# Two heads side by side by columns: values stationary, weighed and transposed maps moving, in three of the four attentions of a 256-token model

## The chip, the core and the metric

The kernel runs on one core of a Trainium2 chip, as one launch. The metric is the device time of the launch in microseconds (us). TensorE (PE in the profile; PEld is its loading of weights) multiplies matrices, VectorE (DVE), ScalarE (ACT) and GpSimd (POOL) work on elements, and SyncE (SP) issues the loads of the weights. Matrix products are written to PSUM, which has 8 banks of 128 partitions by 512 fp32 values.

## The reference

256 tokens of width 1024 pass through four attentions with two MLPs between them; what matters here are the attentions. In A (8 heads, a top-64 selection of keys), B (8 heads, a forget bias) and C (16 heads, two attentions per head over selected and over windowed keys, and a third over 15 compressed blocks) each head has values of width 64. D, a differential attention with values of width 128, follows.

```python
# A, and B in the same form with other logits
p = masked_softmax(logits, valid)                       # per head, queries x keys
o = einsum('bqhk,bqkr->bqhr', p, values)
# C: three attentions of one head are weighed by learned gates
out = gb[..., 0:1] * o_c + gb[..., 1:2] * o_s + gb[..., 2:3] * o_w
```

With 256 tokens, sequence block 0 (queries 0 to 127) sees 128 keys and block 1 (queries 128 to 255) sees 256 keys. A "map" is the matrix of softmax numerators of one head and one attention: both blocks stand in one tile E of 128 queries by 128 + 256 = 384 keys. A and B have 8 maps each, C has 32 and D has 32.

## The kernel before

All matrix products of the projections and of the MLPs run as three passes of rounded fp32 (a value is split into a rounded part, wH or uH, and a remainder, wL or uL). ACT or DVE rounds each weight tile, DVE makes the remainder; both engines do it all the time, for the weights of whatever comes next. The products inside the attentions run in fp32.

The kernel is not written in the order in which it runs. Each part of the work is a generator (a "strand") that yields one operation at a time; a planner (`_Weaver`) keeps a clock for each engine, takes the strand whose operation can begin first (ties by priority), and emits its instruction, so that each engine's instructions stand in the order of that plan. Where a strand yields a list, such as `[act.copy(...), dve.tensor_copy(...)]`, the planner takes the engine on which it would be done first, after adding a toll to DVE (`TOLL1` and `TOLL2`, 1.8 us each, while A, B and C are planned). That comparison counts the operation which an engine has in hand, not what else waits for that engine. Pools are counted as tokens: 8 PSUM banks (B), 8 tiles E, 2 tiles PT, 4 score tokens S, 14 slots of 4 KB per partition.

An attention runs in this order. `maps_strand` (A, B) and `two_maps` (C) compute the scores of two maps into two banks. In A and B two heads of depth 64 stand side by side by rows of the array (`scores2`). `softmax_num` adds the mask and takes the row minimum on DVE (E, nb), and takes the exponential on ACT, which also sums each row (two instructions, 128x128 and 128x256, each with a read of its accumulator). `pv_part` transposes the map on PE (three 128x128 pieces into a bank), ACT copies it to the tile PT, and three matmuls with a piece of PT stationary and the 64 value columns moving add the output, queries on partitions, to the group's bank `ob`. When all maps of a group are there, `finish` divides by the row sums (in C it also multiplies by the gates and adds the two attentions and the compressed one, `oc`), and `o_strand` transposes the result on PE, rounds it (`slot<-bank` CAST on ACT) and makes the remainder on DVE. The transposed and rounded outputs are what `out_proj` multiplies by the output weights, which it may do row by row as the heads arrive. In A and B the last four rows, in C the last row (`LASTC = 1`), come at the end, piece of the output by piece. After `out_proj` the new residual h is transposed and rounded for the MLP (`u_strand`, `split_cols`).

The names in the profile: L113 is the helper through which every ACT, DVE and POOL instruction is made, L341 a matmul, L339 a transposition; `const` in a transposition is the identity. E, PT and sums are as above, `n` is a half-slot of 512 values, `slot` a slot: queries, keys, values, transposed outputs. An fp32 matmul has two records in the profile, one of rounded fp32 or a transposition one.

Of the kernel before, what the change touches and what calls it, by code (L numbers as in the profile page):

```python
# [18 lines left out]
P = 128  # L19
# [242 lines left out]
def tile_kernel(ctx: ExitStack, tc: tile.TileContext, I: dict, out: bass.AP):  # L262
# [6 lines left out]
    slots = ctx.enter_context(tc.tile_pool(name="slots", bufs=14))  # L269
# [4 lines left out]
    NE, NPT, NS = 8, 2, 4  # L274
    W = _Weaver(B=8, E=NE, PT=NPT, S=NS, slot=14, n2=6, raw=3, w=8, rope=2, dup=3)
# [430 lines left out]

    def pv_part(grp, E, v, o0, o1, ne=1):
# [28 lines left out]

    def maps_strand(grp, qs, ks, evs, masks_of, vs, i, prio, bias=None):
        for e in evs:
            yield ("ev", e)
        yield ("acq", "E", 2)  # L740
        Es = [e384("E", NE) for _ in range(2)]
        masks = yield from masks_of(Es)
        yield ("acq", "S", 2)
        yield ("acq", "B", 2)
        bs = [bank(), bank()]
        yield scores2(bs, qs, ks, bias is None)
        if bias:
            yield T(bias(bs))
        grp.start()

        def free(te):
            W.give("B", te)
            W.give("S", te)

        def one(n):
            E = Es[n]
            yield from softmax_num(E, bs[n][:, 0:P], bs[n][:, P:3 * P], masks[n], grp.sums, 2 * (i + n), free)
            yield from pv_part(grp, E, vs[n], ((i + n) * P, (i + n) * P + 64), ((i + n) * P + 64, (i + n + 1) * P))

        W.spawn(one(1), prio + 1, W.end + 0.2)  # L760
        yield from one(0)
# [165 lines left out]
    def layer_ab(pl, hin, hout):  # L927
# [212 lines left out]
        def attention(qT, kT, v, evs, masks_of, bias, side, prio):  # L1140
            for g in range(2):
                def finish(grp, g=g):
                    rs = small(8, "rs", 4)
                    yield dve.reciprocal(out=rs, in_=grp.sums)
                    yield ("acq", "n2")
                    on = n2()
                    te = yield dve.tensor_tensor(
                        out=on.rearrange("p (t h d) -> p h t d", t=2, h=4),
                        in0=grp.ob.rearrange("p (h t d) -> p h t d", h=4, t=2),
                        in1=rs.rearrange("p (h t) -> p h t", h=4).unsqueeze(3).to_broadcast([P, 4, 2, 64]),  # L1150
                        op=ALU.mult)
                    W.give("B", te)
                    yield from o_strand(lambda j, t: on[:, t * S + j * P:t * S + (j + 1) * P],
                                        oH[side][:, 2 * g:2 * g + 2, :], oL[side][:, 2 * g:2 * g + 2, :],
                                        oev[4 * side + 2 * g:4 * side + 2 * g + 2])

                grp = Group(4, finish)
# [46 lines left out]
    def layer_c(pl, hin, hout):  # L1204
# [185 lines left out]
        def cmp_att(g, Q, qev, oc, ocev):  # L1390
# [23 lines left out]
            summed = W.end  # L1414
            rc = small(16, "crc", 2)
            rcev = _Event()

            def sums():
                yield dve.tensor_reduce(out=sc, in_=e3, axis=AX.X, op=ALU.add)
                yield dve.tensor_scalar(out=sc, in0=sc, scalar1=1e-30, scalar2=None, op0=ALU.max)  # L1420
                yield dve.reciprocal(out=sc, in_=sc)
                yield ("ev", gev)
                te = yield dve.tensor_tensor(out=rc.rearrange("p (t h) -> p t h", t=2),
                                             in0=sc.rearrange("p (t h) -> p t h", t=2),
                                             in1=gates[:, :, 8 * g:8 * g + 8, 0], op=ALU.mult)
                rcev.set(te)

            W.spawn(sums(), 8 + 20 * g, summed)
            yield ("acq", "B")
            b = bank()  # L1430
            te = yield T([tr(b[:, t * P:(t + 1) * P], ec[:, t * P:(t + 1) * P]) for t in range(2)])
            yield ("acq", "n2")
            pt = n2()[:, :S]
            te = yield [act.copy(pt, b[:, :S]), dve.tensor_copy(pt, b[:, :S])]
            W.give("B", te)
            yield ("ev", rcev)
            W.give("n2", W.now)
            for t in range(2):
                yield ("acq", "B")
                b = bank()  # L1440
                yield T([mm(b, pt[:, t * P:(t + 1) * P], vBD[g].rearrange("p h d -> p (h d)"), True, True)])
                te = yield dve.tensor_tensor(out=heads(oc[:, t, :]), in0=heads(b),
                                             in1=rc[:, 8 * t:8 * t + 8].unsqueeze(2).to_broadcast([P, 8, 64]),
                                             op=ALU.mult)
                W.give("B", te)
            W.give("n2", te)
            ocev.set(te + 0.16)

        def group(g):
            yield ("acq", "slot", 3)  # L1450
            Q, qev = [kslot(slot(F32R)) for _ in range(2)], [_Event(2), _Event(2)]
            oc = slot().rearrange("p (t n) -> p t n", t=2)
# [34 lines left out]
            ocev = _Event()  # L1487
            W.spawn(cmp_att(g, Q, qev, oc, ocev), 8 + 20 * g)

            def two_maps(grp, q_, j):  # L1490
                for e in qev + kev[0] + kev[1] + vev[0] + vev[1]:
                    yield ("ev", e)
                yield ("acq", "E", 2)
                yield ("acq", "S")
                yield ("acq", "B", 2)
                b1, b0 = bank(), bank()
                yield T([mm(b1, q_[:, P:S], k_[:, g], i == 0, i == 1) for i, k_ in enumerate((kH, kL))]
                        + [mm(b0[:, 0:S], q_[:, 0:P], k_[:, g, :, 0:P], i == 0, i == 1)
                           for i, k_ in enumerate((kH, kL))])
                grp.start()  # L1500
                freed = _Event(2)

                def free(te):
                    freed.set(te)
                    if freed.t is not None:
                        W.give("B", freed.t, 2)
                        W.give("S", freed.t)

                def one(y):
                    E = e384("E", NE)  # L1510
                    yield from softmax_num(E, b0[:, y * P:(y + 1) * P], b1[:, y * S:(y + 1) * S], causal, grp.sums,
                                           4 * j + 2 * y, free)
                    i = 2 * j + y
                    yield from pv_part(grp, E, [vsw[:, t, y, 64 * g:64 * g + 64] for t in range(2)],
                                       (i * P, i * P + 64), (i * P + 64, (i + 1) * P))

                W.spawn(one(1), grp.prio + 2 * j + 1, W.end + 0.2)
                yield from one(0)

            def finish_of(hp):  # L1520
                def finish(grp):
                    rs = small(8, "rs", 4)
                    yield dve.reciprocal(out=rs, in_=grp.sums)
                    yield ("ev", gev)
                    hd = 8 * g + 2 * hp
# [23 lines left out]
            for hp in range(4):  # L1549
                grp = Group(4, finish_of(hp))  # L1550
                grp.prio = 10 + 20 * g + 4 * hp
                for j in range(2):
                    W.spawn(two_maps(grp, Q[j][:, hp, :], j), grp.prio + 2 * j)
# [301 lines left out]
```

## Time and profile before

| | |
|---|---|
| time, three runs | 924.33 to 925.85 us, median 925.32 |
| the profiled execution | 921.53 us, its span 919.4 us |
| PE busy | 901.2 us, 98% of the span |
| DVE, ACT, POOL busy | 586.6, 518.2, 106.4 us |
| mean granted clock of TensorE | 0.998 |

The trace belongs to one execution, 3.8 us below the median of the three runs. Times in it count from the span's start. A's and B's maps are made from about 91 to 130 us, C's from 380 to 457 us, D's from 693 us on. A row of the timeline merges like instructions that follow each other: start, length of the whole row, engine, line, operation, tiles and shapes, count. The start of the next row is a better measure of what a row costs than its own length, since the next instruction begins before the last one's result is written.

### The profile page before, as it was taken

What the parts mean: (1) busy time and instruction counts of PE and PEld (TensorE: products, weight loads), DVE (VectorE), ACT (ScalarE), POOL (GpSimd) and SP (SyncE); (2) the same over time, 40 slices, a digit from 0 to 9 for tenths busy, and PEclk for the clock granted to TensorE, in tenths of its full rate; (3) what the DMA queues carried; (4) which work ended last, traced back from release to release, by engine and by line L of the source; (5) the groups of instructions that cost most, each with busy time, mean ns of one, the idle gap of its engine ahead of it and who ended that gap; (6) DMA issues with size and microseconds to landing.
All of it is one profiled execution on the core that took longest, in us unless ns stands there. A gap on an engine that the chain in (4) does not pass through costs nothing.

```text
span 919.4 us, 14126 instructions
## 1 busy us (share of the span) xinstructions
PE 901.2 (98%) x5196; PEld 766.9 (83%) x5196; DVE 586.6 (64%) x1230; ACT 518.2 (56%) x1025; POOL 106.4 (12%) x149
## 2 busy tenths in 40 slices
PE   8999999999999999999999999999999999999998
PEld 6778888999999878888789999998877778777786
DVE  5688646544454457766654445444878878697781
ACT  5666858455544564787575544455637545274450
POOL 3520000000000051120000000000310503204000
PEclk9999999999999999999999999999999999999999
DMA  7756134655555474312236665655674545544431
GB/s 233 207 178 211 55 104 164 203 183 187 189 191 190 133 249 143 110 46 70 74 123 196 208 192 179 198 184 161 161 220 130 159 138 160 165 133 159 140 115 46
DMA packets 65124, 144.55 MB, mean 157 GB/s; under 512 B 7214, under 2 KB 9744, under 8 KB 65056
## 3 DMA queue, kind: packets, MB, share of 16 engines
q1 hardware_dynamic: 63632, 140.68, 48.0%
q0 software_dynamic: 1424, 2.98, 1.6%
q8 instruction: 41, 0.67, 0.3%
q14 instruction: 27, 0.22, 0.1%
HBM read 142.59 MB, written 1.05 MB: 156 GB/s over the span
## 4 chain that ended last, share of the span: by engine, by line
PE 86%; DVE 4%; POOL 4%; DMA 3%; ACT 1%; issue 1%; SPq 0%; POOLq 0%; DVEq 0%; ACTq 0%
PE bank L341 81%; PE bank L339 5%; POOL qrs L113 2%; DVE wL L113 2%; DVE n L113 1%; DMA h<-in_x_dram 1%; ACT wH L113 1%; DMA raw<-in_c_w_in_dram 1%; POOL T L113 1%; POOL drn L113 1%; DMA raw<-in_ab_w_in_dram 1%; DVE qss L113 0%; DMA raw<-in_l_w_in_dram 0%; ACT n L113 0%; DVE dss L113 0%
## 5 line engine op out<-in xcount | busy, mean ns | idle before, releaser
L113 DVE TENSOR_TENSOR wL<-raw,wH 128x1024 fp32r<-128x1024 f32 (+2 forms) x262 | 317.8, 1214 | 187.9 <-ACT wH L113 186.2
L113 ACT CAST wH<-raw 128x1024 fp32r<-128x1024 f32 (+2 forms) x226 | 234.8, 1041 | 225.4 <-PE bank L341 181.4
L341 PE MATMUL bank<-wH,slot 128*128 128x512 f32 (+1 forms) x784 | 258.3, 396 | 1.2 <-ACT slot L113 0.6
L341 PE MATMUL bank<-wH,uH 128*128 128x512 f32 (+2 forms) x448 | 182.8, 408 | 0.5 <-ACT uH L113 0.5
L341 PE MATMUL bank<-wH,uL 128*128 128x512 f32 (+2 forms) x448 | 174.9, 390 | 0.0
L341 PE MATMUL bank<-wL,uH 128*128 128x512 f32 (+2 forms) x448 | 174.6, 390 | 0.0
L341 PEld LDWEIGHTS bank<-wH,slot 128*128 128x128 f32 x784 | 147.2, 188 | 32.1 <-issue 1.7
L341 PE MATMUL bank<-wL,slot 128*128 128x512 f32 (+1 forms) x392 | 152.7, 390 | 0.0
L341 PE MATMUL bank<-uH,wL 128*128 128x256 f32 x448 | 127.4, 284 | 0.0
L341 PE MATMUL bank<-uL,wH 128*128 128x256 f32 x448 | 127.0, 284 | 0.0
L341 PE MATMUL bank<-uH,wH 128*128 128x256 f32 x448 | 126.1, 281 | 0.0
L341 PEld LDWEIGHTS bank<-wH,uH 128*128 128x128 f32 x448 | 85.1, 190 | 20.2 <-issue 2.3
L341 PEld LDWEIGHTS bank<-wH,uL 128*128 128x128 f32 x448 | 84.8, 189 | 18.7 <-DVE uL L113 0.4
L341 PEld LDWEIGHTS bank<-wL,uH 128*128 128x128 f32 x448 | 85.2, 190 | 15.0 <-DVE wL L113 0.2
L341 PEld LDWEIGHTS bank<-uH,wH 128*128 128x128 f32 x448 | 85.0, 190 | 0.6
L341 PEld LDWEIGHTS bank<-uL,wH 128*128 128x128 f32 x448 | 84.3, 188 | 0.6
L341 PEld LDWEIGHTS bank<-wL,slot 128*128 128x128 f32 x392 | 73.8, 188 | 13.0
L341 PEld LDWEIGHTS bank<-uH,wL 128*128 128x128 f32 x448 | 84.6, 189 | 0.0
L113 ACT ACTIVATE E<-E,nb 128x128 f32<-128x128 f32 (+1 forms) x160 | 70.8, 447 | 9.7 <-DVE nb L113 9.6
L113 POOL TENSOR_TENSOR qrs<-qss,neghalf 128x8 f32<-128x8 f32 x16 | 36.3, 2272 | 141.6 <-DVE dss L113 110.0
L341 PEld LDWEIGHTS bank<-slot,PT 128*128 128x128 f32 x384 | 48.7, 191 | 3.9 <-issue 0.7
L113 POOL TENSOR_TENSOR r<-ms,neghalf 128x1 f32<-128x1 f32 x6 | 4.0, 668 | 403.3 <-DVE ms L113 403.3
(206 smaller groups left out, 953.4 us busy)
## 6 DMA issues: line engine op xcount, KB each, us to landing
raw<-in_mlp_w_dram SPq DMA_DIRECT2D x128, 512.0 KB, 3.9
raw<-in_l_w_in_dram SPq DMA_DIRECT2D x64, 512.0 KB, 3.8
raw<-in_ab_w_in_dram SPq DMA_DIRECT2D x16, 512.0 KB, 4.1
raw<-in_l_w_out_dram SPq DMA_DIRECT2D x16, 512.0 KB, 3.4
raw<-in_c_w_in_dram SPq DMA_DIRECT2D x12, 512.0 KB, 4.0
raw<-in_ab_w_out_dram SPq DMA_DIRECT2D x8, 512.0 KB, 3.4
raw<-in_c_w_out_dram SPq DMA_DIRECT2D x8, 512.0 KB, 3.5
slot<-in_ab_w_in_dram SPq DMA_DIRECT2D x8, 256.0 KB, 6.2
```

The source lines that it names most:

```text
L113: return _Op(self.key, self.cost(name, a, kw), lambda: f(*a, **kw), bank[0] if bank else None)
L339: i = pe.transpose(c[0], c[1], ident[:c[2], :c[2]])
L341: i = pe.matmul(c[0], lhsT=c[1], rhs=c[2], start=c[3], stop=c[4], skip_group_check=True)
```

## The change

It concerns A, B and C; D keeps `pv_part`.

- **The product with the values.** `pv_pair` takes the two maps of two heads (in C: of one attention) together. Their transposed maps are the moving operand (256 columns for the first 128 keys, with both blocks' queries, and 128 columns for the last keys), and the 64 value columns are stationary. Head 0 uses columns 0 to 63 of the array and head 1 columns 64 to 127, so that the output has the head's dimensions on partitions and the queries along the free axis. It is thus already transposed.
- **The division.** Rows are queries in E, but columns in the new output, so the map must be divided before it is transposed: `weigh` multiplies each map by the reciprocal of its row sums (in C also by the gate), two instructions per map, on ACT or DVE. In C the compressed attention's map is weighed too, and its product with the values (`vBD`, 8 matmuls of 256 columns for 4 of 512) is added into the same bank.
- **The end of a group.** `o_round` rounds the bank and takes the remainder; the transposition, the multiplication by reciprocals and, in C, the additions are gone. In C a group now has two pairs of heads, and its end releases two rows of `out_proj` at once (for one before).
- **Buffers.** 4 tiles PT for 2, 13 slots for 14, and C uses no slot for the compressed output.

```diff
-    slots = ctx.enter_context(tc.tile_pool(name="slots", bufs=14))
+    slots = ctx.enter_context(tc.tile_pool(name="slots", bufs=13))
-    NE, NPT, NS = 8, 2, 4
+    NE, NPT, NS = 8, 4, 4
+    def weigh(E, w, ready):
+        for j, (a, z) in enumerate(HALVES):
+            yield [act.activation(out=E[:, a:z], in_=E[:, a:z], func=AF.Copy, scale=w[:, j:j + 1]),
+                   dve.tensor_scalar(out=E[:, a:z], in0=E[:, a:z], scalar1=w[:, j:j + 1], scalar2=None, op0=ALU.mult)]
+        ready.set(W.end + 0.13)
+
+    def pv_pair(grp, Es, ready, vs, col, prio, more=None):
...
+        def across(n):
+            yield ("ev", ready[n])
+            yield ("acq", "B")
+            b = bank()
+            te = yield T([tr(b[:, j * P:(j + 1) * P], Es[n][:, j * P:(j + 1) * P]) for j in range(3)])
+            W.give("E", te)
+            te = yield [act.copy(PTs[n], b[:, :384]), dve.tensor_copy(PTs[n], b[:, :384])]
...
+            o = grp.ob[:, col:col + S]
+            hi = [slice(0, 64), slice(64, 128)]
+            return ([mm(o[hi[n], :], vs[n][0], PTs[n][:, 0:S], first, False) for n in range(2)]
+                    + [mm(o[hi[n], P:S], vs[n][1], PTs[n][:, S:S + P], False, last) for n in range(2)])
+        te = yield T(calls, 2)
...
+        if more:
+            te = yield T([mm(grp.ob[:, col:col + S], more[1], more[2](), False, False)])
...
+    def o_round(grp, H, L, evs):
+        bv = grp.ob.rearrange("p (j q) -> p j q", j=2)
+        yield [act.copy(H, bv), dve.tensor_copy(H, bv)]
+        te = yield dve.tensor_tensor(out=L, in0=bv, in1=H.bitcast(F32), op=ALU.subtract)
...
     def maps_strand(...):     # A, B
+            w = small(2, "w2", 8)
+            yield dve.reciprocal(out=w, in_=sums[:, 2 * n:2 * n + 2])
+            yield from weigh(E, w, ready[n])
...
-                grp = Group(4, finish)
+                grp = Group(2, finish)
...
     def maps_of(grp, hp, prio):     # C, in place of two_maps
+                    w = small(4, "w4", 8)
+                    yield dve.reciprocal(out=w, in_=sums)
+                    yield dve.tensor_tensor(out=wv, in0=wv, op=ALU.mult, in1=gates...)
+                    W.spawn(weigh(Es[1][j], w[:, 2:4], ready[1][j]), prio + 2 * j + 1, W.end + 0.13)
+                    yield from weigh(Es[0][j], w[:, 0:2], ready[0][j])
```

Counted over the whole program, PE loses 144 matmuls `slot,PT` of 64 columns, 32 transpositions `const,n` and 4 matmuls `slot,n` of 512 columns; it gains 48 matmuls `PT,slot` of 256 columns and 48 of 128 columns, each on 64 columns of the array, and 8 matmuls `n,slot` of 256. ACT gains 48 instructions `E<-E,w` of 128x128 and 48 of 128x256: every weighing is on ACT, none on DVE. ACT's 8 casts `slot<-bank` of 128x256 become 4 of 128x512. DVE loses 12 multiplications of 128x512 from the ends of the groups, 4 of the compressed output, and most of the additions, and gains small reciprocals.

PE in the first part of C, before (E and PT are maps, plain and transposed; n_4084 is the compressed attention's transposed map, n_4124 a finished output on its way to be transposed):

```order
L339 MATMUL bank<-const,E 128x128 x6
L341 MATMUL bank<-slot 128x512 x2
L341 MATMUL bank<-slot 128x256 x2
L341 MATMUL bank<-slot,n_4084 128x512
L341 MATMUL bank<-slot,PT 128x64 x6
L339 MATMUL bank<-const,E 128x128 x3
L339 MATMUL bank<-const,n_4124 128x128 x2
```

And in the changed kernel, the same engine and place:

```order
L339 MATMUL bank<-const,E 128x128 x6
L341 MATMUL bank<-slot 128x512 x2
L341 MATMUL bank<-slot 128x256 x2
L341 MATMUL bank<-PT,slot 64x256 x2
L341 MATMUL bank<-PT,slot 64x128 x2
L341 MATMUL bank<-n_4125,slot 128x256
L341 MATMUL bank<-PT,slot 64x256 x2
L341 MATMUL bank<-PT,slot 64x128 x2
```

The six matmuls of a pair of maps have become four, the transposition of the finished output is gone, and the compressed product stands between two pairs.

ACT in the first part of C, before:

```order
L113 ACTIVATE E,sums<-E,nb 128x128
L113 ACTIVATE E,sums<-E,nb 128x256
L113 COPY PT<-bank 128x384 x2
L113 COPY n_4084<-bank 128x256
L113 ACTIVATE E,sums<-E,nb 128x128
L113 ACTIVATE E,sums<-E,nb 128x256
```

ACT in the changed kernel there (w_4143 holds a head's reciprocals times its gates):

```order
L113 ACTIVATE E,sums_4007<-E,nb 128x128
L113 ACTIVATE E,sums_4007<-E,nb 128x256
L113 ACTIVATE slot<-bank 64x4x128 x4
L113 COPY PT<-bank 128x384 x2
L113 ACTIVATE E<-E,w_4143 128x128 x2
L113 ACTIVATE E<-E,w_4143 128x256 x2
L113 ACTIVATE E,sums_4027<-E,nb 128x128
L113 ACTIVATE E,sums_4027<-E,nb 128x256
```

Four weighings (two maps) have come in between the copies of one pair and the exponentials of another. In A and B 32 such instructions are added, in C 64.

PE at the end of C, before (wH,slot and wL,slot are `out_proj`):

```order
L341 MATMUL bank<-slot,PT 128x64 x6
L341 MATMUL bank<-wH,slot 128x512
L341 MATMUL bank<-wL,slot 128x512
L341 MATMUL bank<-wH,slot 128x512 x2
L341 MATMUL bank<-wL,slot 128x512
L341 MATMUL bank<-wH,slot 128x512
L339 MATMUL bank<-const,n_4907 128x128 x2
L341 MATMUL bank<-wH,slot 128x512
```

PE at the end of C in the changed kernel:

```order
L339 MATMUL bank<-const,E 128x128 x12
L341 MATMUL bank<-PT,slot 64x256 x2
L341 MATMUL bank<-PT,slot 64x128 x2
L341 MATMUL bank<-n_4471,slot 128x256
L341 MATMUL bank<-PT,slot 64x256 x2
L341 MATMUL bank<-PT,slot 64x128 x2
L341 MATMUL bank<-wH,slot 128x512
L341 MATMUL bank<-wL,slot 128x512
L341 MATMUL bank<-wH,slot 128x512 x2
```

Before, 6 of `out_proj`'s matmuls stand between the last product and the last transposition, and 12 behind it, with the transpositions of h between them. In the changed kernel all that is left, 24 matmuls, stands behind the last product, and then 16 transpositions of h in one piece. At the end of A and B, 57 matmuls of `out_proj` stand behind the last transposition of an output before, and 42 behind the last product in the changed kernel. Of the rounding casts of weights, ACT has 7 between the first exponential of A and the last cast of B for 5 before, and 6 in that stretch of C for 9 before. Between the end of A's selection mask and the first exponential there is one cast of weights on ACT for two before.

## Rows read from the trace of the kernel before

**Rows 1.** The page's part 1: busy us, share of the span, instructions.
```profile
PE 901.2 (98%) x5196; PEld 766.9 (83%) x5196; DVE 586.6 (64%) x1230; ACT 518.2 (56%) x1025; POOL 106.4 (12%) x149
```
**Rows 2.** Busy time by window: stretch, length, PE, PEld, DVE, ACT, POOL, clock, DMA.
```profile
90.70:129.90 39.20, 39.20 (x279) 33.35 (x278) 23.10 (x94) 29.90 (x91) 0.00 (x0) 1.00 0.22 67
380.30:457.30 77.00, 74.96 (x508) 65.47 (x507) 53.82 (x210) 58.82 (x187) 7.81 (x14) 1.00 0.19 62
380.30:394.30 14.00, 13.99 (x98) 12.07 (x98) 12.18 (x62) 13.71 (x56) 0.73 (x1) 1.00 0.12 39
```
**Rows 3.** Timeline of PE in C: start, length, engine, line, operation, count.
```profile
395.59 1.45 PE L341 MATMUL bank<-slot,PT 128*128 128x64 f32 x12
396.88 0.83 PE L339 MATMUL bank<-const,E 128*128 128x128 f32 x6
397.46 0.94 PE L341 MATMUL bank<-slot 128*128 128x512 f32 x4
```
**Rows 4.** Timeline of PE in B, and at the end of `out_proj`.
```profile
106.21 0.93 PE L341 MATMUL bank<-slot 64*128 64x128 f32 x8
107.07 0.62 PE L341 MATMUL bank<-cumk,slot 72*128 72x384 f32 x2
...
143.49 0.39 PE L341 MATMUL bank<-wH,uH 128*128 128x512 f32 x1
143.72 0.39 PE L341 MATMUL bank<-wL,uH 128*128 128x512 f32 x1
```
**Rows 5.** Timeline of ACT in C.
```profile
386.26 0.39 ACT L113 ACTIVATE E<-E,nb 128x128 f32<-128x128 f32 x1
386.56 0.19 ACT L113 ACTIVATION_READ_ACCUMULATOR E<-E,nb 128x1 f32 x1
386.65 0.49 ACT L113 ACTIVATE E<-E,nb 128x256 f32<-128x256 f32 x1
387.05 0.19 ACT L113 ACTIVATION_READ_ACCUMULATOR E<-E,nb 128x1 f32 x1
387.14 0.83 ACT L113 COPY PT<-bank 128x384 f32<-128x384 f32 x2
387.87 0.38 ACT L113 COPY n<-bank 128x256 f32<-128x256 f32 x1
388.13 0.41 ACT L113 ACTIVATE E<-E,nb 128x128 f32<-128x128 f32 x1
```
**Rows 6.** ACT's groups, 380.3 to 457.4 us: busy, mean ns, idle before, releaser.
```profile
L113 ACT CAST wH<-raw 128x1024 fp32r<-128x1024 f32 x9 | 9.4, 1045 | 3.9 <-PE bank L341 3.7
L113 ACT CAST slot<-bank 128x256 fp32r<-128x256 f32 x8 | 2.9, 368 | 1.9 <-PE bank L339 1.8
L113 ACT ACTIVATE slot<-bank 64x512 fp32r<-64x512 f32 x4 | 2.4, 590 | 1.8 <-PE bank L339 1.7
L113 ACT ACTIVATE n<-bank,r 128x512 f32<-128x512 f32 x2 | 1.4, 684 | 0.2 <-PE bank L341 0.2
L113 ACT ACTIVATE n<-n 128x256 f32<-128x256 f32 x2 | 0.8, 414 | 0.2 <-DVE n L113 0.2
L113 ACT COPY n<-bank 128x256 f32<-128x256 f32 x2 | 0.7, 374 | 1.1 <-PE bank L339 1.1
```
**Rows 7.** ACT's groups, 90.7 to 129.95 us.
```profile
L113 ACT CAST slot<-bank 128x512 fp32r<-128x512 f32 x4 | 2.3, 582 | 0.1
```
**Rows 8.** Timeline of ACT at the start of A's exponentials.
```profile
88.05 1.05 ACT L113 CAST wH<-raw 128x1024 fp32r<-128x1024 f32 x1 [1.74 <-DVE slot L113]
90.72 0.40 ACT L113 ACTIVATE E<-E,nb 128x128 f32<-128x128 f32 x1 [1.62 <-DVE nb L113]
```
**Rows 9.** Timeline of all engines behind C: the last cast, and PE.
```profile
456.97 0.36 ACT L113 CAST slot<-bank 128x256 fp32r<-128x256 f32 x1
...
458.71 0.73 PE L341 MATMUL bank<-wH,slot 128*128 128x512 f32 x2 [0.59 <-DVE slot L113]
...
464.43 0.50 PE L341 MATMUL bank<-wH,uH 128*128 128x512 f32 x1 [0.51 <-ACT uH L113]
```

More of the change, by code (lines that the diff above doesn't have):

```diff
@@ L273, in tile_kernel @@
     psum = ctx.enter_context(tc.tile_pool(name="psum", bufs=8, space=PSUM))
[L274 to L275 removed]
+    NE, NPT, NS = 8, 4, 4
+    W = _Weaver(B=8, E=NE, PT=NPT, S=NS, slot=13, n2=6, raw=3, w=8, rope=2, dup=3)
     act, dve, pool = _Engine("A", nc.scalar), _Engine("D", nc.vector), _Engine("P", nc.gpsimd)
@@ L705, in start, with calls @@
                 self.sums = small(8, "sums", 6)
+    def weigh(E, w, ready):
[4 more added lines that the diff above has]
+    def pv_pair(grp, Es, ready, vs, col, prio, more=None):
+        yield ("ev", ready[0])
+        yield ("acq", "PT", 2)
+        PTs = [e384("PT", NPT) for _ in range(2)]
+        there = _Event(2)
+        def across(n):
[5 more added lines that the diff above has]
+            te = yield [act.copy(PTs[n], b[:, :384]), dve.tensor_copy(PTs[n], b[:, :384])]
+            W.give("B", te)
+            there.set(te + 0.2)
+        W.spawn(across(1), prio + 0.1, W.now)
+        yield from across(0)
+        yield ("ev", there)
+        if more:
+            yield ("ev", more[0])
+        if not grp.opening:
+            grp.opening = True
+            yield ("acq", "B")
+            grp.ob = bank()
+            grp.opened.set(W.now)
+        else:
+            yield ("ev", grp.opened)
+        def calls():
+            first, last = grp.done == 0, grp.done == grp.n - 1
+            o = grp.ob[:, col:col + S]
[3 more added lines that the diff above has]
+        te = yield T(calls, 2)
+        W.give("PT", te, 2)
+        if more:
+            te = yield T([mm(grp.ob[:, col:col + S], more[1], more[2](), False, False)])
+            more[3](te)
+        grp.done += 1
+        if grp.done == grp.n:
+            W.spawn(grp.finish(grp), FIN, te + 0.2)
@@ L735, in pv_part @@
             W.spawn(grp.finish(grp), FIN, te + 0.2)
[L737 to L761, printed above, removed]
     def o_strand(nat, H, L, evs, gp=None, width=2):
@@ L1142, in finish @@
                 def finish(grp, g=g):
[L1143 to L1155, printed above, removed]
-                grp = Group(4, finish)
+                    yield from o_round(grp, oH[side][:, 2 * g:2 * g + 2, :], oL[side][:, 2 * g:2 * g + 2, :],
+                                       oev[4 * side + 2 * g:4 * side + 2 * g + 2])
+                grp = Group(2, finish)
                 for j in (0, 2):
@@ L1492, in two_maps @@
                     yield ("ev", e)
[L1493 to L1515, printed above, removed]
@@ new lines, in maps_of @@
+                W.spawn(head(1), prio + 2, W.now)
+                for y in range(2):
+                    vs = [[vsw[:, t, y, 64 * g:64 * g + 64] for t in range(2)]] * 2
+                    more = None
+                    if y == 0:
+                        more = (pcev, vBD[g][:, 2 * hp:2 * hp + 2, :].rearrange("p h d -> p (h d)"), lambda: pc[0], used)
+                    W.spawn(pv_pair(grp, Es[y], ready[y], vs, (hp % 2) * S, prio + y, more), prio + y)
+                yield from head(0)
@@ L1561, in layer_c @@
         yield from out_proj(pl["out"], opnd, lambda k: oev[k], residual(hout), LASTC)
-        W.give("slot", W.end, 14)
+        W.give("slot", W.end, 12)
     def plan_d():
```

141 lines of the change are left out of this document (81 added, 60 removed).

## The prediction

> **What bounds the kernel now.** I read the page's busy shares first, then windows of the two stretches that the change touches, then the timelines of PE and ACT inside them, and last ACT's groups. The shares show PE busy for 98% of the span, DVE for 64%, ACT for 56% [rows 1]. Over the whole program ACT looks like an engine with much room. The windows show something else. While A's and B's maps run (90.7 to 129.9 us) PE is busy all 39.20 us, and ACT 29.90; while C's run, PE is busy 74.96 of 77.00 us and ACT 58.82; in the first 14 us of C, ACT is busy 13.71, as full as PE [rows 2]. The clock is 1.00 in all of them, so it plays no part. PE sets the time in both stretches, but ACT has only 9.3 and 18.2 us left, and the change takes work from PE and hands it to ACT. Two steps follow: what PE saves, and whether ACT can pay.
>
> **PE's step.** A pair of maps now takes twelve records of 64 moving columns, from 395.59 to 396.88, 1.29 us; the six transpositions behind them take 0.58, 0.097 each [rows 3]. There are 24 pairs, so 24 x 1.29 = 31.0 us go, and 32 transpositions of outputs with 32 x 0.097 = 3.1 us. What comes is 24 pairs of two matmuls of 256 columns and two of 128, each on half of the array's columns. The trace has no halves by columns. It has a pair with the same moving shapes in halves by rows: eight records, 0.86 us [rows 4]. Bounds: a pass of 512 columns costs 0.23 us [rows 4]. If the halves overlap wholly, four passes of 128 + 256 = 384 columns cost 4 x 384/512 x 0.23 = 0.69; if they follow each other, and each half has the overhead of the row halves, it is twice 0.86, 1.72. I take 0.86, the row with the same shapes: 24 x 0.86 = 20.6 us. The compressed product, 8 matmuls of 256 columns for 4 of 512, costs the same. The sum is 20.6 - 31.0 - 3.1 = -13.5 us, if PE remains what is waited for.
>
> The halves by rows run beside each other, since 0.86 lies far nearer to 0.69 than to 1.72 [rows 4]. The Trainium skill says so too (TensorEngine Tiling (Array Packing), Key Properties), and adds that changing the tiling mode drains TensorE; by that the excess over 0.69 would be the drain. The same page's section PSUM Bottleneck speaks against the change: tiling speeds TensorE but not the emptying of what it writes, for which both ScalarE and VectorE should be used. Here all 96 weighings go to one of them, and ACT's 13.71 of 14.00 us is what this rule looks like in a row [rows 2].
>
> **ACT's step.** A map costs ACT at present two exponentials with their reads, 386.26 to 387.14, 0.88 us, and one copy to PT, half of 387.14 to 387.87, 0.37 us [rows 5]. New is the weighing: two instructions of 128x128 and 128x256 from tile to tile. The trace has no multiplication of that form. The nearest rows are the exponentials of the same shapes, tile to tile with an operand per partition: 0.30 and 0.40 us to the start of their reads [rows 5], 0.70 together. A lower bound is the copy of 128x256, 387.87 to 388.13, 0.26 us [rows 5], which with a smaller one of about half makes 0.40; an upper one the exponentials with their reads, 0.88. I take 0.70, the shape, route and operand being the same.
>
> By the Trainium skill (ScalarE: Activation LUTs, What ACT_TABLE_LOAD costs) a pass can be built from a fixed part, a part per element and one per pointer operand; my estimate from its figures is 0.29 + 0.40 = 0.69 us per map, so the trace's 0.70 agrees and the sum stays. Its section Rules for kernel authors gives multiplications to VectorE, the opposite of what the order does here; no row of before shows a weighing there.
>
> So a map will cost 0.88 + 0.37 + 0.70 = 1.95 us.
>
> - A and B: 16 maps x 1.95 = 31.2; 7 casts of weights of 1.05 [rows 8] = 7.4; 4 casts of outputs of 0.58 = 2.3 [rows 7]; two banks of 128x512 scaled by an operand per partition, 1.4 as the two of that form in C [rows 6]. Sum 42.3 us, for a stretch of 39.2.
> - C: 32 x 1.95 = 62.4; 6 casts x 1.05 = 6.3; 4 roundings of 128x512 at 0.58 = 2.3 for the eight of 0.37; 2.4 for the four of 64x512; 1.4 + 0.8 + 0.7 = 2.9 for the compressed maps [rows 6]. Sum 76.3 us, for a stretch of 77.0.
>
> ACT becomes the bound in both. It will not be full to the last: where it is full today 0.29 of 14.00 us, 2.1%, stay idle [rows 2], 0.9 and 1.6 us. At the end of a stretch nothing is left to it but to wait for the last pair: six transpositions (0.58) and a product (0.86), 1.4 us. So 2.3 us idle in A and B, 3.0 in C.
>
> **Where the waits go.** ACT works in order. Four weighings now stand before the exponentials of the next maps [the order at the start of C]. Those exponentials empty no bank (E is a tile), but the transpositions of their maps wait for them and then for their own weighing, and the copies to PT, which give banks back, wait behind both. PE has the next scores and `out_proj` to fill in with, until banks or E run out; then it stands, for ACT, about as long as the change saves it. DVE, with 53.82 of 77.00 us [rows 2], loses work and is not waited for more than now.
>
> **Sum by place.**
> - A and B: one cast fewer stands before the first exponential (two from before 88.05 to 90.72 now, 1.05 each [rows 8]), so it starts 1.1 us earlier. The last cast comes at 42.3 + 2.3 - 39.2 - 1.1 = +4.3 us. Behind it 42 matmuls of `out_proj` stand for 57, 15 x 0.23 = 3.5 us less [rows 4]. Net +0.8.
> - C: the last cast comes at 76.3 + 3.0 - 77.0 = +2.3 us. Behind it stand 24 matmuls for 12, as the last group releases two rows: 12 x 0.23 = +2.8. The remainder on DVE is of twice the columns; PE waits 0.59 for it today [rows 9], and I add 0.2, the difference between the two sizes of cast. The way from the last cast to the MLP's first matmul, 456.97 + 0.36 to 464.43, is 7.1 us [rows 9] and becomes 10.1. Net +5.3.
> - D, the MLPs: their instructions stand as before but for small shifts: 0. One slot fewer and two PT more: 0 while PE is not the bound. If slots were short, the weights' loads would be late, which I leave in the range.
>
> That is +6.1 us: 921.5 + 6.1 = 927.6 for the profiled execution. It lies 3.8 us below the median of the runs, so the time is 931.4 us.
>
> **Rivals.**
> 1. *ACT keeps up.* Casts of weights, of which there are 13 in the two stretches, yield to the maps, and ACT's idle 9.3 and 18.2 us [rows 2] take the weighings as they are. Then PE stays the bound and the time is 925.3 - 13.5 = 911.8. For it: the small share of ACT on the page. Against it: 16 and 32 maps x 0.70 = 11.2 and 22.4 us are more than ACT has free. It decides if a map's weighing costs under about 0.3 us, or if ACT's other work moves to DVE. Chance 0.13. This is the one on the other side.
> 2. *The weighing is cheap.* At 0.40 a map ACT needs 37.5 and 66.7 us. The last casts come at 37.5 + 0.8 + 1.4 - 39.2 - 1.1 = -0.6 and 66.7 + 1.4 + 1.4 - 77.0 = -7.5; with -3.5 and +3.0 behind them the sum is -8.6, the time 916.7. For it: the copy of 0.26 us. Against it: the copy has no operand per partition. Chance 0.13.
> 3. *The column halves do not run beside each other.* The change then does not do what it says: a pair costs 1.72, PE 24 x 1.72 - 34.1 = +7.2 us; PE is the bound again, and with the +3.0 behind C the time is 935.5. For it: no row shows halves by columns, and both write the same bank. Against it: the row halves. Chance 0.12.
>
> **How the numbers follow.** The forecast has 0.62. Its own range is 925 to 940: below by the idle ends being filled and 24 matmuls partly hidden (6 us), above by 0.88 us a weighing, 48 x 0.18 = 8.6 us more. What a measurement of this kernel can tell from no change is about 0.2%, 1.85 us, so 923.5 to 927.2 count as the same. Faster: rivals 1 and 2 and a sliver of the forecast, 0.27. Same: 0.11, from the forecast's low end and between the cases. Slower: 0.62. For 8 in 10 I take 915 to 941, which holds rival 2 at its price and rival 3, and leaves out rival 1.
>
> **What will show it.** ACT should be busy for nearly all of both stretches, and PE idle there behind PT's copies and the weighed E, for 10 us or more in all. The weighings should cost 0.30 and 0.40 us from start to start, a pair's product 0.86, the last cast of C should come near 459.3 us and the MLP's first matmul 10 us behind it. I am wrong in PE's step if a product of a pair takes over 1.3 us; in ACT's price if a map's weighing takes under 0.5; in the bound if PE is still busy over 97% of both stretches; and in the ends if the gap behind C's last cast stays near 7 us.

## The result and the profile after

The changed kernel takes 932.07 us (931.45 to 936.38, 5 runs) against 924.55 us of before (922.24 to 925.85, 5 runs). The ratio is 1.009, 95% interval 1.0062 to 1.0118: slower by 6 to 11 us. The forecast was 931.4 us, +6.1 us. The profiled execution of the changed kernel took 936.38 us, 4.3 above its median; a second profile, of 931.79 us, is among the experiments.

The page of the changed kernel, busy us, share of the span and instructions, to be read against [rows 1]:

```profile
PE 903.5 (97%) x5076; PEld 751.8 (80%) x5076; DVE 578.0 (62%) x1223; ACT 547.9 (59%) x1116; POOL 100.5 (11%) x143
```

On the page alone little has happened: ACT has 30 us more, PE is as busy as before in a longer span. The windows of the two stretches tell more (stretch, length, PE, PEld, DVE, ACT, POOL, clock, DMA share and GB/s, as in [rows 2]), from A's first exponential to the end of B's last cast, and the same in C:

```profile
90.19:136.10 45.91, 41.91 (x254) 28.84 (x252) 24.63 (x104) 42.07 (x125) 0.00 (x0) 1.00 0.21 69
389.00:468.85 79.85, 71.47 (x423) 52.71 (x422) 41.44 (x191) 75.93 (x244) 3.25 (x8) 0.96 0.10 31
```

ACT has become the fullest engine in both: 42.07 of 45.91 and 75.93 of 79.85 us. PE, full before, has holes, and DVE is busy for half the time. (PE's 41.91 us in A and B are close to ACT's, but they are not what PE needs there: with the weighing on DVE, below, 248 records take 37.89 us for these 254.) In C the DMA share has fallen from 0.19 to 0.10. That fits ACT's six casts of weights there for nine; with the weighing on DVE the share is 0.19 again. Two groups of ACT in C, the new weighings (busy, mean ns of one, idle before):

```profile
L113 ACT ACTIVATE E<-E,w 128x256 f32<-128x256 f32 x32 | 14.7, 505 | 0.0
L113 ACT ACTIVATE E<-E,w 128x128 f32<-128x128 f32 x32 | 11.3, 403 | 0.3 <-DVE w L113 0.2
```

ACT's timeline late in C (start, length of the row, count), where four weighings, two maps, start at 463.05 and the next instruction at 464.45:

```profile
463.05 1.51 ACT L113 ACTIVATE E<-E,w 128x128 f32<-128x128 f32 x4
464.45 1.05 ACT L113 CAST wH<-raw 128x1024 fp32r<-128x1024 f32 x1
```

That is 1.40 us for two maps, 0.70 a map. On PE a pair's product, the form that no row of before had, stands between 459.35 and 460.15:

```profile
459.35 0.87 PE L341 MATMUL bank<-PT,slot 128*64 128x256 f32 x8
460.15 0.70 PE L341 MATMUL bank<-n,slot 128*128 128x256 f32 x2
```

0.80 us for eight records, where twelve took 1.29 [rows 3] and the halves by rows 0.86 [rows 4]. What PE waited for in A's and B's stretch, and then in C's (us in total, times, longest):

```profile
PE bank L341 <- ACT PT L113: 1.5, 2, 1.0
PE bank L339 <- ACT E L113: 1.3, 2, 0.7
PE bank L341 <- ACT slot L113: 0.3, 1, 0.3
```
```profile
PE bank L339 <- DVE n L113: 2.7, 1, 2.7
PE bank L339 <- ACT E L113: 2.1, 4, 1.1
PE bank L341 <- ACT PT L113: 1.6, 3, 1.0
PE bank L341 <- DVE slot L113: 1.2, 2, 0.8
```

Before, PE was busy all of A's and B's stretch [rows 2], and in C it waited for this:

```profile
PE bank L341 <- ACT PT L113: 0.6, 1, 0.6
PE bank L339 <- DVE slot L113: 0.5, 1, 0.5
PE bank L339 <- DVE n L113: 0.4, 1, 0.4
```

Now five of the seven rows name ACT, with 6.8 of 10.7 us, 6.5 of them for the weighed E and its copy PT. The longest single wait, though, 2.7 us near the start of C, is for DVE and the compressed attention's map n, which the change divides before it is transposed.

Behind A and B, PE meets something that the forecast did not have. Its timeline, in part, from its first wait at the end of B on:

```profile
128.89 0.44 PE L339 MATMUL bank<-const,E 128*128 128x128 f32 x2 [0.68 <-ACT E L113]
...
130.42 0.86 PE L341 MATMUL bank<-PT,slot 128*64 128x256 f32 x6 [0.52 <-ACT PT L113]
...
132.47 0.44 PE L339 MATMUL bank<-const,E 128*128 128x128 f32 x2 [0.60 <-ACT E L113]
133.87 1.25 PE L341 MATMUL bank<-PT,slot 128*64 128x256 f32 x8 [0.96 <-ACT PT L113]
136.15 0.79 PE L341 MATMUL bank<-wH,slot 128*128 128x512 f32 x1 [1.03 <-ACT slot L113]
136.74 0.63 PE L341 MATMUL bank<-wL,slot 128*128 128x512 f32 x1
...
139.82 0.63 PE L341 MATMUL bank<-wL,slot 128*128 128x512 f32 x1
140.25 0.63 PE L341 MATMUL bank<-wH,slot 128*128 128x512 f32 x1
140.68 1.05 PE L339 MATMUL bank<-const,h 128*128 128x128 f32 x4
```

A pass of 512 columns takes 0.43 us (from 139.82 to 140.25, and to 140.68), not the 0.23 of [rows 4]: the granted clock is 0.78 on the mean of 130 to 140 us, so part of it ran at 1.2 GHz instead of 2.4. Ahead of it stand PE's waits of 0.5 to 1.0 us from 128 us on.

Behind C, the timelines of PE, of DVE and of ACT:

```profile
475.13 0.39 PE L341 MATMUL bank<-wH,slot 128*128 128x512 f32 x1
477.60 2.45 PE L339 MATMUL bank<-const,h 128*128 128x128 f32 x16 [2.07 <-DVE h L113]
481.02 0.50 PE L341 MATMUL bank<-wH,uH 128*128 128x512 f32 x1 [0.97 <-ACT uH L113]
```
```profile
474.35 2.59 DVE L113 TENSOR_TENSOR wL<-raw,wH 128x1024 fp32r<-128x1024 f32 x2 [1.64 <-ACT wH L113]
476.86 2.48 DVE L113 TENSOR_TENSOR h<-bank,h 128x512 f32<-128x512 f32 x4
```
```profile
473.27 1.05 ACT L113 CAST wH<-raw 128x1024 fp32r<-128x1024 f32 x1 [1.81 <-DMA raw<-in_mlp_w_dram]
474.63 1.05 ACT L113 CAST wH<-raw 128x1024 fp32r<-128x1024 f32 x1 [0.31 <-DMA raw<-in_mlp_w_dram]
```

PE is done with `out_proj` at 475.5, but DVE has two remainders of weights in front of the residuals h, and those had waited for ACT's casts of weights. Four such casts stand behind C's last cast of an output, where before there was none, and they wait for their weights to arrive, 4.2 us in all. So h begins at 476.86 and PE's 16 transpositions at 477.60.

### The profile page after: what moved, and what is told of

It reads as the page before. It is cut to its first block, busy times and chain, and to the rows that moved or that the text cites. A ratio compares the mean times of both kernels' runs of the same rounds, so it can differ in the third digit from the quotient of the medians.

```text
span 934.3 us, 13917 instructions
## 1 busy us (share of the span) xinstructions
PE 903.5 (97%) x5076; PEld 751.8 (80%) x5076; DVE 578.0 (62%) x1223; ACT 547.9 (59%) x1116; POOL 100.5 (11%) x143
## 3 DMA queue, kind: packets, MB, share of 16 engines
q1 hardware_dynamic: 63632, 140.68, 47.4%
## 4 chain that ended last, share of the span: by engine, by line
PE 84%; ACT 5%; DVE 4%; POOL 3%; DMA 2%; issue 2%; SPq 0%; POOLq 0%; ACTq 0%
PE bank L341 79%; PE bank L339 4%; ACT E L113 2%; ACT wH L113 1%; POOL qrs L113 1%; DMA raw<-in_mlp_w_dram 1%; DVE wL L113 1%; POOL T L113 1%; DVE n L113 1%; DMA h<-in_x_dram 1%; DMA raw<-in_c_w_in_dram 1%; ACT n L113 1%; ACT PT L113 1%; ACT slot L113 0%; DVE E L113 0%
## 5 line engine op out<-in xcount | busy, mean ns | idle before, releaser
L341 PEld LDWEIGHTS bank<-uL,wH 128*128 128x128 f32 x448 | 84.3, 188 | 0.6
L113 POOL TENSOR_TENSOR qrs<-qss,neghalf 128x8 f32<-128x8 f32 x16 | 33.9, 2122 | 142.2 <-DVE dss L113 110.3
L341 PE MATMUL bank<-slot 64*128 64x128 f32 (+3 forms) x288 | 39.8, 348 | 0.3 <-ACT PT L113 0.3
```

The source lines that it names most:

```text
L113: return _Op(self.key, self.cost(name, a, kw), lambda: f(*a, **kw), bank[0] if bank else None)
L341: i = pe.matmul(c[0], lhsT=c[1], rhs=c[2], start=c[3], stop=c[4], skip_group_check=True)
```

## The experiments

The theory going in: ACT's list is what PE waits for (theory 1). Its rivals: the ends of the stretches cost the time wherever the weighing runs (theory 2), or DVE would be the next bound (theory 3). Every ratio is to the kernel before, run on the same chip. The table gives, from the profile of each kernel, the way from the first exponential to the end of the last cast of an output, and from there to the MLP's first matmul, for A with B and for C, in us.

| kernel | median us | ratio (95%) | A, B | behind | C | behind |
|---|---|---|---|---|---|---|
| before | 924.55 | | 39.2 | 13.6 | 77.0 | 7.1 |
| forecast | 931.4 | | 44.6 | 10.1 | 79.3 | 10.1 |
| changed | 932.07 | 1.009 (1.006 to 1.012) | 45.9 | 14.4 | 79.9 | 12.2 |
| changed, again | 931.92 | 1.0103 (1.008 to 1.013) | 45.8 | 14.5 | 79.6 | 12.1 |
| weighing on DVE | 912.27 | 0.9882 (0.986 to 0.990) | 37.9 | 12.4 | 70.1 | 8.7 |
| no weighing | 911.15 | 0.9871 (0.985 to 0.989) | 37.4 | 13.1 | 67.5 | 8.7 |
| weighing halved | 919.12 | 0.9967 (0.994 to 0.9995) | 40.1 | 11.7 | 75.5 | 8.7 |
| C row by row | 931.0 | 1.0082 (1.006 to 1.010) | 46.0 | 13.2 | 79.8 | 9.1 |
| DVE, row by row | 914.05 | 0.9896 (0.986 to 0.993) | 37.9 | 12.4 | 73.2 | 6.2 |
| PE kept busy | 930.54 | 1.0071 (1.005 to 1.009) | 45.9 | 12.0 | 77.6 | 11.8 |
| C only | 936.01 | 1.0143 (1.012 to 1.017) | 46.4 | 12.7 | 77.2 | 11.8 |
| C only, 14 slots, 2 PT | 936.29 | 1.0127 (1.011 to 1.015) | 39.2 | 13.6 | 84.3 | 10.5 |
| changed, 14 slots, 2 PT | 936.13 | 1.0134 (1.011 to 1.016) | 43.4 | 12.1 | 84.5 | 12.1 |
| DVE, 14 slots, 2 PT | 918.37 | 0.9944 (0.993 to 0.996) | 34.5 | 13.8 | 73.0 | 9.3 |

The rest of the program varies too: before A's first exponential by 4.7 us over these profiles, and in the projections of C, from their first matmul to the first exponential, between 53.3 and 61.5 us, with stretches at half clock that are not the same from kernel to kernel. So a stage is read from the table, and a whole kernel from its ratio.

**The weighing on DVE.**

```diff
-            yield [act.activation(out=E[:, a:z], in_=E[:, a:z], func=AF.Copy, scale=w[:, j:j + 1]),
-                   dve.tensor_scalar(out=E[:, a:z], in0=E[:, a:z], scalar1=w[:, j:j + 1], scalar2=None, op0=ALU.mult)]
+            yield dve.tensor_scalar(out=E[:, a:z], in0=E[:, a:z], scalar1=w[:, j:j + 1], scalar2=None, op0=ALU.mult)
```

> All 96 weighings of A, B and C on DVE, none on ACT; nothing else changed by hand. Theory 1 (ACT's list is what PE waits for): ACT loses 0.70 us a map, 11.2 us in A and B and 22.4 us in C, of lists that were busy 39.3 of 42.8 and 74.2 of 78.0 us in the changed kernel; PE's idle time between A's first exponential and the last product (2 us in A and B, 8 us in C) goes, and with it the half clock behind it; the time is 914 to 922 us. Theory 2 (what costs is the end of each stretch, the work that waits for the last output, wherever the weighing runs): less than 3 us come back, 929 to 932 us. Theory 3 (DVE, which makes minimum, mask and remainder in order, becomes the wait): no gain, 930 us or more, with PE waiting for E from DVE.

912.27 us, below theory 1's range: 20 us under the changed kernel and 1.2% under the kernel before. Its windows of the same two stretches:

```profile
90.65:128.54 37.89, 37.89 (x248) 27.18 (x247) 30.49 (x135) 30.04 (x92) 0.00 (x0) 1.00 0.25 78
377.66:447.80 70.14, 66.47 (x423) 49.59 (x422) 57.44 (x257) 56.32 (x182) 3.52 (x8) 1.00 0.19 61
```

PE is full again in A and B, the clock 1.00 in both, and DVE and ACT carry nearly the same, 57.44 and 56.32 us in C. DVE's own weighings are cheaper too; its timeline and its groups in C:

```profile
431.01 1.00 DVE L113 TENSOR_SCALAR E<-E,w 128x128 f32<-128x128 f32 x4
431.93 0.28 DVE L113 CUSTOM_DVE_ANT_0 E<-bank,const 128x128 f32<-128x128 f32 x1
```
```profile
L113 DVE TENSOR_SCALAR E<-E,w 128x256 f32<-128x256 f32 x32 | 10.0, 343 | 0.0
L113 DVE TENSOR_SCALAR E<-E,w 128x128 f32<-128x128 f32 x32 | 8.4, 297 | 0.2
```

Four take 0.92 us, 0.46 a map, for ACT's 0.70. Theories 2 and 3 fall.

**No weighing.**

```diff
-            yield [act.activation(out=E[:, a:z], ...), dve.tensor_scalar(out=E[:, a:z], ...)]
+            yield from ()
```

> The weighing is left out (the maps are not divided; the reciprocals are still made). Theory 1 (ACT's list): the time falls to the bound by PE, 911 to 918 us, at or a little under the run with the weighing on DVE, and PE is busy over 97% of both stretches with a clock of 1.00 in them. Theory 2 (the ends of the stretches): the time stays over 927 us, since the ends are as they were. Theory 3 (DVE): much lower than the run with the weighing on DVE.

911.15 us, only 1.1 us under the weighing on DVE. This is what the rest of the change is worth, its buffers and its ends included: 1.3% of 923.24 is 11.9 us (10.0 to 13.8), beside the 13.5 that the forecast gave PE's step alone. PE is busy all the time from 90 to 130 us, and in C it still lacks 0.6 to 0.8 us in three windows of 10.

**C row by row.**

```diff
-            for gp in range(2):
-                grp = Group(4, finish_of(gp))
-                for hp in (2 * gp, 2 * gp + 1):
+            for gp in range(4):
+                grp = Group(2, finish_of(gp))
+                for hp in (gp,):
...
```

`o_round`, the column offset of `pv_pair` and `finish_of` are made to fit one pair of heads.

> In C a group has one pair of heads again, and its end releases one row of out_proj (four groups of two products for two of four, eight roundings of 128x256 for four of 128x512); the weighing stays on ACT. Theory 1 as the forecast had it: the way from the last cast of C to the MLP's first matmul, 12.2 us in the changed kernel's trace, falls by 12 matmuls x 0.23 = 2.8 us and more, to 8 to 9.5 us; ACT's list hardly changes, so the time is 928 to 930 us. Rival (ACT's list sets where the stretch ends, and the matmuls of out_proj only move from behind it into PE's idle time before it, with casts of weights delayed the more): within 1 us of 932.

Behind C 9.1 us stand for 12.2: the forecast's term of 3.0 us for two rows at once is right in the stage. The 12 matmuls run inside the stretch before, which stays at 79.8 us with them. The profiled execution, 929.02 us, is 2.8 us under that of the changed kernel's second profile. Over all runs, though, 931.0 us is in the rival's range and cannot be told from 931.9, so the saving is not shown in the total.

**The change in C only.**

```diff
...
-                grp = Group(2, finish)
+                grp = Group(4, finish)
```

With it, `maps_strand` and the end of a group in A and B (`finish`) are those of the kernel before.

> A and B as before (the map divided at the group's end), C changed; 13 slots and 4 PT as in the changed kernel. By the forecast's split (A and B +0.8, C +5.3 us over the kernel before) the time is 930 to 931 us. By the one profile of the changed kernel, where the first MLP starts 7.0 us later than before and the second a further 9.6 us later, A's and B's part goes and C's stays: first MLP near 143.5 us, and the time 3 to 6 us under the changed kernel, 926 to 929 us.

A miss for both splits: 936.0 us, slower than the whole change. A and B with their old code take 59.1 us from the first exponential to the MLP, 46.4 and 12.7, where the same code took 52.8. Only the buffers differ there, 13 slots and 4 PT.

**The buffers.** The same kernel with 14 slots and 2 PT:

```diff
-    slots = ctx.enter_context(tc.tile_pool(name="slots", bufs=13))
+    slots = ctx.enter_context(tc.tile_pool(name="slots", bufs=14))
-    NE, NPT, NS = 8, 4, 4
+    NE, NPT, NS = 8, 2, 4
...
```

> As the run with the change in C only, but with 14 slots and 2 PT as before, so that A's and B's instructions stand word for word as in the kernel before. Theory A (one slot fewer re-plans B's projections, and this is what put the first MLP at 149.5 us in the run with C only, for 143.5): the first MLP is back near 143.5 us and the time is 6 to 8 us under that run, 928 to 930 us, which leaves C with a loss of 5 to 7 us, near the forecast's +5.3. Theory B (the loss in that run came from the C stretch alone): within 2 us of it, 934 to 938 us.

A and B are back at 39.2 and 13.6, but C's stretch grows to 84.3 us, and the time stays at 936.3. So theory A holds for the stage and fails for the total. The whole change with these buffers:

> The whole change with the weighing on ACT, but 14 slots and 2 PT. Theory A (the slot costs A and B time in the changed kernel too): first MLP at 145 to 148 us for 150.5, time 926 to 930 us. Theory B (in the changed code ACT's list sets A's and B's end whatever the buffers): first MLP near 150 us, time within 2 us of 932.

The same again: A and B 55.4 us for 60.3, C's stretch 84.5 for 79.9 (at a clock of 0.90 for 0.96, so that part of it may be the clock), and the time, 936.1 us, fits neither theory. Over three pairs of runs that differ in the buffers alone, the third of them below, 14 slots with 2 PT take 2 to 6 us less in A and B and 3 to 7 us more in C's stretch, and the change's choice paid one for the other. No run changed slots and PT one at a time, so which of the two does what is not shown.

**DVE and row by row together.** Both edits shown above.

> The weighing on DVE and C's groups of one pair of heads together. If the 2.8 us of the forecast for the 12 further matmuls behind C hold where ACT is not the bound, the time is 909 to 911 us, 1.5 to 3 us under the run with the weighing on DVE alone, and the MLP's first matmul comes 8 to 9 us behind the last cast of C. Rival: the end of C is set by the remainders of weights on DVE, not by out_proj's matmuls: 912 to 914 us.

914.05 us, the upper end of the rival's range, though not for its reason. Behind C 2.4 us are saved (6.2 for 8.7), but the stretch in C is 3.1 us longer, with four more roundings and groups. What makes it longer was not tried.

**PE kept busy.**

```diff
+    def filler():
+        yield ("acq", "B")
+        b = bank()
+        while rounded[0] < 4:
+            te = yield T([mm(b[:, :256], warmth[:, :P], warmth, True, True)])
+            yield ("at", te + 0.08)
+        W.give("B", te)
...
+        if made[0] == 8:
+            W.spawn(filler(), 5000, W.end)
```

> The changed kernel, with some 36 matmuls of a tile of zeros (128x256, bf16, into a bank of their own) put into PE's waits between B's last scores and its last rounding; they add nothing to any result. In the changed kernel's trace PE is busy 6.83 of the 10 us from 130 to 140, the clock is 0.78 there and 0.88 in the next 10, and out_proj's passes take 0.43 us for 0.23. Theory C (the half clock behind PE's wait costs some 3 us): the clock stays at 1.00 there, the first MLP comes at 147 to 148 us for 150.5, and the time is 928 to 930 us. Rival (out_proj waits for its operands and weights anyway): first MLP near 150, time 931 to 934.

The windows 130 to 140 us of the changed kernel, and of this one:

```profile
130.00:140.00 10.00, 6.83 (x28) 4.30 (x29) 4.80 (x6) 5.73 (x11) 0.00 (x0) 0.78 0.78 246
```
```profile
130.00:140.00 10.00, 9.06 (x59) 6.44 (x58) 4.97 (x5) 5.35 (x10) 0.00 (x0) 1.00 0.75 247
```

The clock is 1.00 for 0.78. The stretch before is the same, 45.9 us, and the way behind it 12.0 for 14.4: the half clock cost some 2.4 us there (the same 42 matmuls, in an order planned anew). What is left of PE's timeline at the join, at full clock:

```profile
136.24 0.40 PE L341 MATMUL bank<-wL,slot 128*128 128x512 f32 x1
137.28 0.73 PE L341 MATMUL bank<-wH,slot 128*128 128x512 f32 x2 [0.64 <-DVE slot L113]
```

Over the whole kernel 930.54 us is 1.5 us under the changed one, with intervals that overlap, so the gain is shown in the stage, not in the total. C's order was planned anew behind it, and its clock is 1.00; which of the two makes its 77.6 us is not shown.

**The changed kernel again.**

> The changed kernel once more, for a second profile: its first one was of an execution of 936.4 us, 4.3 above its own median, with the clock at 0.77 to 0.93 in 360 to 375 and 389 to 420 us. Theory C (those low clocks belong to that execution): from C's first exponential to the MLP's first matmul 88.5 to 90.5 us for 92.0, near the forecast's 89.4, and A's and B's way from the first exponential to the first MLP stays at 58 to 61 us, for 52.8 before and 54.7 by the forecast. Rival (the stage itself is longer than the forecast): 91 us or more in C at a clock of 1.00.

The windows of its two stretches:

```profile
88.39:134.17 45.78, 41.91 (x254) 28.84 (x252) 24.63 (x104) 42.08 (x125) 0.00 (x0) 1.00 0.21 69
384.41:464.00 79.59, 70.01 (x423) 51.27 (x422) 41.43 (x191) 75.93 (x244) 3.25 (x8) 0.98 0.10 30
```

The stage lengths repeat within 0.3 us, though the clock in C is 0.98 for 0.96: ACT sets the stretch, and PE's clock matters little in it. The rival is right for C, 91.7 us to the MLP's first matmul, and A's and B's way is 60.3 us again. What differs is ahead of C, 53.9 us for 56.7, where the first profile had its clock at 0.77.

**The weighing halved.**

```diff
+            yield dve.tensor_scalar(...) if j else act.activation(...)
```

> In each map ACT weighs the 128x128 part and DVE the 128x256 part, so that ACT keeps 0.30 of 0.70 us a map: 4.8 us in A and B, 9.6 in C. Theory 1 (ACT's list, in proportion): ACT's lists come to 42.3 - 6.4 = 35.9 and 76.3 - 12.8 = 63.5 us, under what PE needs (39.4 and 68.3 us busy or waiting in the run with the weighing on DVE), so nearly the whole gain is there: 912 to 917 us. Rival (each weighing on ACT stands in the way of exponentials and copies, whatever the list's sum; the gain goes by the share moved, 57%): 919 to 923 us.

919.12 us, within the rival's range and outside theory 1's. A and B have most of the gain (from 45.8 to 40.1, where DVE has 37.9), C less than half (from 79.6 to 75.5, where DVE has 70.1). C's window, and two of PE's waits in it:

```profile
381.67:457.14 75.47, 68.81 (x423) 50.89 (x422) 52.09 (x225) 65.75 (x214) 3.17 (x8) 0.98 0.19 61
```
```profile
PE bank L341 <- ACT PT L113: 2.9, 5, 1.0
PE bank L339 <- ACT E L113: 1.8, 1, 1.8
```

ACT is busy for 65.75 us, less than PE's 68.81, and PE still waits 4.7 us for it. So ACT's price does not vanish once its list is shorter than PE's, and the sum of the list is not the whole account. That each weighing on ACT delays the exponential behind it by its length would fit, but no run shows it by itself.

**DVE with the old buffers.** The edit on DVE with 14 slots and 2 PT.

> The weighing on DVE with 14 slots and 2 PT. In the changed kernel with the old buffers the way from A's first exponential to the first MLP was 55.4 us for 60.3. Theory A (a slot more is worth something where PE is the bound too): that way falls under 50.3 us, and the time is 907 to 911 us. Rival (2 PT let only one pair be between copy and product, so that PE waits for PT, above all in C): 913 to 918 us.

918.37 us, just above the rival's range. Theory A is right for the way in A and B, 48.3 us for 50.3, and not for the total: C's stretch takes 73.0 us for 70.1, though none of PE's waits in it is for PT as the rival had it, and the projections ahead of C 61.5 for 55.0 in this profile, with the clock at 0.50 to 0.67 in its windows from 345 to 365 us. Why the clock fell there was not tried.

## Why the prediction was right, and where it was not

**What becomes the bound: right.** ACT's list was forecast at 42.3 and 76.3 us and measures 42.07 and 75.93; the price of 0.70 us a map is met to the hundredth, and the last casts come 45.9 and 79.9 us behind the first exponentials, for 44.6 and 79.3. That the weighing on ACT is what costs is shown by the weighing on DVE (-20 us) and by leaving it out (-21 us). ACT's idle time in the stretches was 3.8 and 3.9 us for 2.3 and 3.0. The halved weighing sets a limit to the account by lists: with a list shorter than PE's, ACT still made PE wait.

**PE's step: right in sign, near in size.** A pair takes 0.80 us for 0.86, and without the weighing the whole change saves 10.0 to 13.8 us, for 13.5 from PE's step. That the halves by columns run beside each other (rival 3) is settled by the same row. The prediction's 1.72 for halves one after the other was twice the 0.86 itself, so it could not test the row halves; the figure to set 0.86 and 0.80 against is eight passes of 384 columns for its four, 2 x 0.69 = 1.38 us by its own working, and both lie far under that.

**What PE waits for: right in part.** PE was to be idle "behind PT's copies and the weighed E, for 10 us or more in all". It was idle 4.0 and 8.4 us, of which the waits for these two make 6.5. And DVE was to be "not waited for more than now": in C PE waits 3.9 us for it, 2.7 of them for the compressed map, where before it waited 0.9.

**The start of A: misread.** One cast fewer on ACT was to bring A's first exponential forward by 1.1 us. But ACT stood idle for 1.62 us in front of it, for DVE [rows 8], so the cast was not what it waited for. It came 0.5 and 2.3 us earlier in the two profiles, within what this start varies by over all profiles (4.7 us).

**Behind A and B: wrong.** The step was "Behind it 42 matmuls of `out_proj` stand for 57, 15 x 0.23 = 3.5 us less [rows 4]. Net +0.8." It gave 10.1 us and 14.4 were measured. Some 2.4 us of the difference are the half clock, which the prediction had ruled out ("so it plays no part"): that was read from stretches in which PE stood for 2 of 116 us, and the change made it wait. With PE kept busy the way is still 12.0 us: 42 x 0.23 = 9.7, the 12 transpositions of h that stand before the MLP's first matmul about 1.1, and 0.6 of waiting for the remainder make 11.4 of it. The forecast's difference of counts did not carry over, as the 57 had been counted from the last transposition of an output and the 13.6 us from its cast. Before, PE and ACT there:

```profile
128.68 0.60 PE L339 MATMUL bank<-const,n 128*128 128x128 f32 x4
129.03 0.48 PE L341 MATMUL bank<-wH,slot 128*128 128x512 f32 x1
129.35 0.39 PE L341 MATMUL bank<-wL,slot 128*128 128x512 f32 x1
129.58 0.62 PE L341 MATMUL bank<-wH,slot 128*128 128x512 f32 x2
130.04 0.40 PE L341 MATMUL bank<-wL,slot 128*128 128x512 f32 x1
```
```profile
129.31 0.59 ACT L113 CAST slot<-bank 128x512 fp32r<-128x512 f32 x1
```

Four of the 57, 0.9 us, begin before the cast ends at 129.90 and so are no part of the 13.6. Behind them `out_proj` runs on while DVE makes the remainder, where in the changed kernel nothing is left to do meanwhile and PE waits.

**Behind C: the term right, one wait missing.** 12 further matmuls and the longer rounding were to cost 3.0 us, and undoing them gives 3.0 (12.2 to 9.1) or 2.4 (8.7 to 6.2). The missing 2.1 us are PE's wait for h, 2.07 us, behind remainders of late weights: with the weighing on DVE, where 24 matmuls follow the last cast as well, PE does not wait for h and the way is 8.7 us. The prediction saw ACT giving up casts of weights but not who would wait for them.

**The buffers: wrong, and hidden by each other.** "One slot fewer and two PT more: 0 while PE is not the bound" stands against 2 to 6 us lost in A and B and 3 to 7 us won in C, by both buffers together.

**The total.** The four stretches grew by 15 us, twice the 7.2 that their terms came to. The number was met because other stretches of the two later profiles were 0.6 to 4.9 us shorter in sum, and because the profile of before was of an execution some 3 us under its median. That other part varies from one execution to the next, and no run here settles how much of it belongs to the change. So the sign and the mechanism rest on rows, and the agreement to 1 us is partly chance.

**Where the weighing went.** All 96 weighings went to ACT, with DVE at 41.44 of 79.85 us. The Trainium skill (ScalarE: Activation LUTs, Rules for kernel authors) gives multiplications to VectorE. Here 0.46 us a map on DVE for 0.70 on ACT agrees with it. The place counted more than the price: in C 32 x 0.70 = 22.4 us are taken from the full engine, and 32 x 0.46 = 14.7 put on the half empty one. The prediction also set ACT's 13.71 of 14.00 us beside a rule on emptying PSUM; but a weighing goes from E to E and empties no bank, so these rows say nothing on that rule.

## What to carry to other kernels

When work leaves the bounding engine, add up the list of the engine that receives it stage by stage: ACT's 56% of the program before became only 59%, but 92 and 95% of the two stretches that mattered. A planner that compares only the operation in hand, with a fixed toll of 1.8 us on DVE, put all 96 weighings on the wrong side, which made a loss of 0.9% of what is a gain of 1.2% with the weighings on DVE; no run changed the toll by itself. And when PE is made to wait, look behind the wait: here its clock and the weights that were not prepared meanwhile cost again after it.

## What the runs showed that was not expected

Column halves of 64 columns with moving shapes of 256 and 128 columns took 0.80 us a pair, 0.06 less than row halves of the same moving shapes. And PE's waits between 128 and 136 us, none longer than 1.03 us and with short products between them, were followed by passes of 0.43 us for some 6 us; with 36 matmuls of zeros in those waits the passes took 0.23.
